# One more VA/GA pair by block products in the input projection of a hybrid decoder trunk

## The chip, the cores and the metric

The kernel runs on one core of one Trainium2 chip. The metric is device time in microseconds for one execution. TensorE (PE) does the matmuls; its weight loads are counted as PEld. VectorE (DVE) and ScalarE (ACT) work element by element, GpSimd (POOL) issues the DMAs that add to what is in memory already, and SyncE (SP) issues nearly all other DMAs. Each engine, and each queue of DMA issues, works through its own instructions in order.

## The reference

One layer over 1024 positions of width 1024, in float32. A projection `w_in` of 7168 columns is cut into six parts, of which `va` and `ga` (1024 columns each) are what the change is about:

```python
h = rms_norm(x, g_mix[l])
z = jnp.einsum("bsd,de->bse", h, w_in[l]) + b_in[l]
va, ga, xb, gb, sa, sb = jnp.split(z, cuts, axis=-1)

u = va * jax.nn.sigmoid(ga)
u = causal_depthwise_conv(u, conv_a_w[l], conv_a_b[l])      # 31 taps
u = jax.nn.silu(layer_norm(u, ln_g[l], ln_b[l]))
y_a = jnp.einsum("bsc,cd->bsd", u, w_a_out[l])

v = causal_depthwise_conv(xb, conv_b_w[l], conv_b_b[l])     # 4 taps
v = rg_lru(v, ...)                                          # two gates by head, a linear recurrence
y_b = jnp.einsum("bsc,cd->bsd", v * jax.nn.gelu(gb), w_b_out[l])

m = jax.nn.sigmoid(sa) * y_a + jax.nn.sigmoid(sb) * y_b
x = x + jnp.einsum("bsd,de->bse", m, w_o[l])
```

A squared-ReLU MLP of width 4096 and a last RMSNorm follow.

## The kernel before

**Two halves for each operand.** A float32 operand is used as a high part in the matmul's own format and a low part, the rest. A product of two operands takes three matmuls: high·high, high·low, low·high. Splitting costs an ACT copy for the high part and, for the low part, either a DVE subtraction or an ACT copy with a minus sign and a POOL DMA that adds the source (`split_dma`, lines 63 to 68).

**The first part** computes columns of `w_in` in chunks of 128 channels by 1024 positions, in the order of the list `CH`: all of XB (12 chunks), and pairs VA j, GA j for j below `NJ` = 7. A chunk is 8 blocks of depth, 3 matmuls, 2 halves of the positions: 48 matmuls of 128x128 by 512. Between the chunks lie the 16 heads' gate matmuls of the recurrence (four groups of four heads). Step `s` issues chunk `s`, and the work on chunk `s` − 1: for XB the convolution of width 4, for VA and GA the sigmoid (`u_gate`, ACT) and the product (`u_value`, DVE). Every 31-tap convolution is one list of 48 DVE operations (`conv`), which begins with two ACT operations (lines 635, 636).

**The second part** computes the other chunks of `w_in` in pairs of chunks, by Strassen's scheme in Winograd's form: the pair's two channel blocks, the two halves of the depth and the two halves of the positions make a 2 by 2 block product that takes 7 block products in place of 8. A block product is 12 matmuls (`z_mm`). Products 1, 2, 3 use blocks of x as they are, products 4 to 7 use sums of blocks, which are made once, early in the first part (`x_sum`, `x_make`), stored to DRAM, and loaded again late (`x_get` loads both halves of a split sum; `x_raw` loads a sum as it is, into the tile of its low half, and `x_split` then splits it: one ACT copy, one DVE subtraction for each of two blocks of 128x1024). The left operands are blocks and sums of the weights (`z_load`, `z_sums`, `z_lhs`). `ZPAIRS` gives the order of 15 pairs: `s`, `t`, `g` are parts of SA, SB, GB, and `u7` is the pair VA 7, GA 7. `zseq` gives the order of products: (pair, product).

**What sets the order.** The order on each engine is that of the program. Step n of the second part issues, in this order: what ACT and DVE do with the result of product n − 1 (`z_post`) and n − 2 (`z_post2`), product n (PE), the left operand of product n + 4, the weight sums of product n + 5, then what `ZX[n]` lists. DVE work passes through a list (`later`), which is emitted at the end of the step sorted by the time at which the planner takes it to be ready; gaps that the planner's clocks show are filled with taps of a convolution (`fill`). `taps["hold"]` keeps it from starting the next convolution. `XS[s]` lists extra work of the first part's steps.

**The recurrence's last group** (tiles 9, 10, 11) is finished around the border of the two parts: `scan_exp` (ACT: exp and tanh), `scan_root` (ACT: square root), `scan_in` and `scan_tile` (DVE; a scan tile is three long operations).

**Tiles.** Blocks of 128x1024 float32 (the sums, their halves, gates, the convolutions' inputs and results) come from one pool of 37. A DMA or engine that needs a tile waits until one is free.

**After the second part** come the projections `w_b_out`, `w_a_out` and `w_o`, and the MLP. In the first steps of the MLP (`GX`, from line 1690 on) `up_lhs(i, p)` makes a left operand, and `g_post` at line 1395 copies the result of a first product out of PSUM (`u`, `u_late`), before the second product may add to it.

```python
z_get(n - 1, z_post)
z_get(n - 2, z_post2)
...
z_get(n, z_mm)
z_get(n + 4, z_lhs)
if n > 0:
    z_get(n + 5, z_sums)
if n < L:
    for f, *a in ZX.get(n, ()):
        f(*a)
vector_work(clk["P"] - 0.3)
```

Of the kernel before, what the change touches and what calls it, by code (L numbers as in the profile page):

```python
# [31 lines left out]
def trunk_kernel(ctx: ExitStack, tc: tile.TileContext, x, xt_in, xt_eo, vecs, w_in, w_a_out, w_b_out,  # L32
# [383 lines left out]
    VA, GA, XB, GB, SA, SB = 0, 8, 16, 28, 40, 48  # L416
# [150 lines left out]
    def scan_in(ready, *ts):  # L567
        for t in ts:
            later(ready, 1.2, nc.vector.tensor_tensor, gate[1, t], gate[1, t], vt.pop(t), ALU.mult)
# [23 lines left out]
    def u_value(j, psv, ready=0):  # L593
        uv = ut[j].rearrange("p (o n) -> p o n", o=2)
        later(ready, 1.28, nc.vector.scalar_tensor_tensor, uv,
              psv.rearrange("p (n o) -> p o n", o=2), bin_c[:, VA + j:VA + j + 1], uv,
              ALU.add, ALU.mult)
        fresh.append(j)
# [108 lines left out]
        later(at("A", 1.06), 1.2, nc.vector.tensor_tensor, l, l.bitcast(F32), xbh[p][c2].bitcast(F32),  # L707
              ALU.subtract)

    NJ = 7  # L710
    CH = [XB + 0, VA + 0, GA + 0, XB + 1, XB + 2, VA + 1, GA + 1, XB + 3, XB + 4, XB + 5, VA + 2, GA + 2, XB + 6, XB + 7, XB + 8, VA + 3, GA + 3, XB + 9, XB + 10, XB + 11, VA + 4, GA + 4, VA + 5, GA + 5, GA + 6, VA + 6]
    NC1 = len(CH)
    zps = {n: z0[n] for n in range(N0)}
    wraw, wst = {}, {}
# [6 lines left out]
    def vector_work(end):  # L721
        for ready, _, cost, f, a in sorted(todo, key=lambda x: x[:2]):
            dve(cost, ready, f, *a)
        todo.clear()
        taps["wait"] += fresh
        fresh.clear()
        fill(end)
# [10 lines left out]
    def chunk_mm(s, n0, n1, halves=(0, 1), low_last=False):  # L738
# [13 lines left out]

    ZPAIRS = [{"u": lambda i: (VA + i, GA + i)}.get(
        t[0], lambda i, c={"g": GB, "s": SA, "t": SB}.get(t[0]): (c + 2 * i, c + 2 * i + 1))(int(t[1]))
        for t in "s0 s1 g0 g1 g2 s2 s3 u7 g3 g4 g5 t0 t1 t2 t3".split()]
    NZ = len(ZPAIRS)
    zraw, zs, zo, zb = {}, {}, {}, {}
    zn = [0]
# [28 lines left out]
    def z_lhs(i, p):  # L787
# [9 lines left out]
        else:  # L797
# [2 lines left out]
        zo[i, p] = o  # L800


    zseq = [(0, 1), (1, 1), (0, 2), (1, 2), (0, 6), (0, 7), (1, 7), (0, 5), (1, 6), (0, 3), (0, 4),
            (1, 5)]
    for i in range(2, NZ):
        zseq += [(i, 1), (i, 7), (i - 1, 4), (i, 6), (i, 2), (i - 1, 3), (i, 5)]
    zseq[-7:] = [(NZ - 1, p) for p in (1, 7, 6)] + [(NZ - 2, 4), (NZ - 1, 2), (NZ - 1, 5), (NZ - 2, 3)]
    zseq += [(NZ - 1, 3), (NZ - 1, 4)]

# [1 line left out]
    for i in range(2, NZ):  # L811
        n = zseq.index((i, 1))
        ZL[n - 9] = ((z_load, i, 0),)
        ZL[n - (6 if i > 2 else 4)] = ((z_load, i, 1),)
    def z_get(n, f):
# [5 lines left out]
    head_at = {s: n for n, s in enumerate(HS0)}  # L821

    EXP = {head_slot: g for g, head_slot in enumerate(HS0[4 * g + 3] + 1 for g in range(3))}
    RAW = (4, 5)
    XS = {4: ((x_sum, 0),), 5: ((x_make, 0, 5), (x_make, 0, 7)), 6: ((x_make, 0, 6), (x_make, 0, 4), (x_sum, 1)),
          7: tuple((x_make, 1, p) for p in (5, 7, 6, 4)),
          NC1 - 3: ((scan_exp, 3),), NC1 - 2: ((x_get, 0, 6), (x_get, 1, 6)),
          NC1 - 1: ((scan_in, 0, 9, 10, 11), (scan_root, 3), (x_get, 0, 7), (x_get, 1, 7))}
    w_load(3)
    head_w(0)  # L830
    w_load(4)
# [1 line left out]
    with tc.manual_schedule(engines=ENGINES):  # L833
        for s in range(3, NC1):
            w_load(s + 2)
            taps["hold"] = s > NC1 - 4
            begun = clk["P"]
            clk["A"], clk["V"] = max(clk["A"], begun + 0.5), max(clk["V"], begun - 2)

# [165 lines left out]
    def z_h(i, m_, hf):  # L1005
        t = ZPAIRS[i][m_] - GB
        if 0 <= t < 12:
            hb[t, hf] = h = EV(f"hb{t}_{hf}")
            nc.sync.dma_start(h, hd[t, :, HALVES[hf]])
# [23 lines left out]
    def z_post2(i, p):  # L1033
# [3 lines left out]
        elif p == 4:  # L1037
            z_out(i, 1, 0, zb[i, "u"], "c")

    ZX = {0: ((x_raw, 0, 5), (x_raw, 1, 5)), 1: ((later, 0, 4.8, scan_tile, 9),), 2: ((x_split, 0, 5),), 3: ((x_split, 1, 5),),  # L1040
          4: ((later, 0, 4.8, scan_tile, 10), (x_raw, 0, 4), (x_raw, 1, 4)), 6: ((x_split, 0, 4),), 7: ((x_split, 1, 4),),
          9: ((later, 0, 4.8, scan_tile, 11),)}
    H_AT = {2: (0, 0), 5: (1, 1), 3: (0, 1), 4: (1, 0)}
    with tc.manual_schedule(engines=ENGINES):

# [37 lines left out]
        z_get(2, z_lhs)  # L1083
        z_get(3, z_lhs)
        u_value(NJ - 1, zps[NC1 - 1])
        vector_work(clk["V"])
        z_h(0, 0, 0)
        for n in range(len(zseq) + 2):
            for f, *a in ZL.get(n, ()):
                f(*a)  # L1090
            if n >= L:
                for f, *a in ZX.get(n, ()):
                    f(*a)
            taps["hold"] = n < 6
            if n >= 20 and n % 6 == 2:
                sum_up(clk["P"], 1)
            clk["A"], clk["V"] = max(clk["A"], clk["P"] + 0.5), max(clk["V"], clk["P"] - 2)
            z_get(n - 1, z_post)
            z_get(n - 2, z_post2)
            if n + 3 < len(zseq):  # L1100
                i, p = zseq[n + 3]
                if p in H_AT:
                    z_h(i, *H_AT[p])
# [8 lines that stand above are left out]
# [581 lines left out]
    def g_get(n, f):  # L1693
# [31 lines left out]
        3: ((x1_normed, 0, 1), (x1_normed, 1, 1), (g_t, "u", 0, 1), (g_t, "u", 1, 1)),  # L1725
        4: ((g_t, "u", 0, 2), (g_t, "u", 1, 2)), 5: ((g_parts, "u", 6, 0), (up_lhs, 0, 6)),
        6: ((g_parts, "u", 6, 1), (up_lhs, 1, 6), (g_parts, "u", 5, 0), (up_lhs, 0, 5)),
        7: ((g_parts, "u", 5, 1), (up_lhs, 1, 5), (g_t, "u", 0, 3), (g_t, "u", 1, 3)),
        9: ((g_parts, "u", 7, 0), (up_lhs, 0, 7)), 10: ((g_parts, "u", 7, 1), (up_lhs, 1, 7)),
        11: ((g_parts, "u", 3, 0), (g_t, "u", 0, 4), (g_parts, "u", 3, 1), (g_t, "u", 1, 4))}.items()})  # L1730
    with tc.manual_schedule(engines=ENGINES):
        for j in range(8):
# [162 lines left out]
    with tc.manual_schedule(engines={mybir.EngineType.Activation, mybir.EngineType.DVE,  # L1895
                                     mybir.EngineType.PE}):
        for n in range(len(useq)):
# [4 lines left out]
            while ready < min(len(useq), n + look + 1):  # L1902
                i, p = useq[ready]
# [289 lines left out]
```

## Time and profile before

| | us |
|---|---|
| median of 3 runs | 1542.22 |
| lowest and highest | 1541.28, 1542.23 |
| the profiled execution, its own time | 1542.07 |
| its span, first to last instruction | 1540.30 |
| PE busy | 1530.1 |
| DVE busy | 1228.9 |
| ACT busy | 911.2 |
| POOL busy | 184.7 |

Times in the views count from the start of the span. The first part runs to about 339 us, the second from there to about 627 us. A row of a timeline gives the start, the length, the engine, the line, the operation, the tiles (out<-in), the shapes and a count; in square brackets stands how long the engine was idle before it, and what ended that. A row of the chain gives start, length, and the work that the end of the program hung on at that time. In the list of waits the numbers are the total in us, the number of waits, and the longest. A window's row gives the busy time of PE, PEld, DVE, ACT and POOL with their counts of instructions, the granted clock of PE, the mean busy share of the DMA engines and GB/s.

### The profile page before, as it was taken

Reading aid. Unit: us, or ns where it says so; the run is one execution under the profiler, and the core shown is the slowest. Engines: PE = TensorE matmul, PEld = TensorE weight load, DVE = VectorE, ACT = ScalarE, POOL = GpSimd, SP = SyncE. Lnnn points to the kernel's source line nnn. Section 1 sums busy time; section 2 is a strip of 40 time slices with the busy share of each in tenths; the row PEclk is TensorE's granted clock in tenths of the full one; section 3 lists DMA queues with packets and bytes.
Section 4 is the critical chain, followed back from the end, with each engine's and each line's share of the span. In section 5 each row is a group of like instructions: output and inputs, shape, how many; then the busy total and the mean of one; then the engine's idle time right before and its main releaser. Section 6 shows DMA issues by size and latency. Waiting matters only on the chain.

```text
span 1540.3 us, 19049 instructions
## 1 busy us (share of the span) xinstructions
PE 1530.1 (99%) x6765; PEld 1258.2 (82%) x6765; DVE 1228.9 (80%) x1660; ACT 911.2 (59%) x1270; POOL 184.7 (12%) x221
## 2 busy tenths in 40 slices
PE   9999999999999999999999999999999999999998
PEld 7888888788888888888888887888888888888886
DVE  6999988989999998478568879765555558888897
ACT  6758576667676676435375777444444475555553
POOL 0000000012222221000022332000000011111110
PEclk9999999999999999999999999999999999999999
DMA  7575554699998888844579898523333779888852
GB/s 295 115 235 149 149 145 116 159 280 244 255 249 214 219 225 253 272 172 128 187 194 304 191 194 201 195 82 132 114 116 108 241 212 232 223 225 222 204 125 110
DMA packets 133504, 296.02 MB, mean 192 GB/s; under 512 B 20896, under 2 KB 38944, under 8 KB 133408
## 3 DMA queue, kind: packets, MB, share of 16 engines
q1 hardware_dynamic: 102016, 215.10, 41.5%
q0 software_dynamic: 30672, 77.35, 27.5%
q10 hardware_dynamic: 720, 2.36, 0.4%
q8 instruction: 53, 0.87, 0.2%
q14 instruction: 43, 0.35, 0.1%
HBM read 155.03 MB, written 60.82 MB: 140 GB/s over the span
## 4 chain that ended last, share of the span: by engine, by line
PE 97%; DMA 1%; ACT 1%; DVE 1%; issue 0%; SPq 0%; POOL 0%; DVEq 0%; POOLq 0%; ACTq 0%
PE z L749 16%; PE d L1946 15%; PE yb L1165 8%; PE e L2063 3%; PE keep L1946 2%; PE z L257 2%; PE rg L529 1%; PE rg L531 1%; PE rg L530 1%; DMA w_raw<-in_w_dram 1%; DMA xc<-in_xt_dram 0%; PE z4a L948 0%; PE go2e L1341 0%; PE z4e L948 0%; PE z2e L948 0%; PE z3e L948 0%
## 5 line engine op out<-in xcount | busy, mean ns | idle before, releaser
L749 PE MATMUL z<-xh,win_h 128*128 128x512 f32 x368 | 115.0, 390 | 0.0
L1958 DVE TENSOR_TENSOR acc<-acc,d 128x1024 f32<-128x1024 f32 x72 | 87.8, 1220 | 33.4 <-PE d L1946 32.7
L749 PE MATMUL z<-xl,win_h 128*128 128x512 f32 x368 | 113.5, 389 | 0.0
L749 PE MATMUL z<-xh,win_l 128*128 128x512 f32 x368 | 91.8, 391 | 0.0
L653 DVE SCALAR_TENSOR_TENSOR y<-u,vec,y 128x511 f32<-128x511 f32 (+14 forms) x120 | 88.4, 737 | 0.0
L653 DVE SCALAR_TENSOR_TENSOR y<-yt,csum,y 128x511 f32<-128x511 f32 (+6 forms) x112 | 82.6, 738 | 0.0
L653 DVE SCALAR_TENSOR_TENSOR yt<-u,vec,yt 128x511 f32<-128x511 f32 (+6 forms) x112 | 82.6, 737 | 0.0
L749 PEld LDWEIGHTS z<-xh,win_l 128*128 128x128 f32 x368 | 69.1, 188 | 15.6
L749 PEld LDWEIGHTS z<-xh,win_h 128*128 128x128 f32 x368 | 69.0, 188 | 15.3 <-ACT win_h L68 0.4
L541 ACT ACTIVATE g<-rg,vec 96x1024 f32<-96x1024 f32 x32 | 35.7, 1115 | 77.0 <-PE rg L531 76.3
L749 PEld LDWEIGHTS z<-xl,win_h 128*128 128x128 f32 x368 | 69.1, 188 | 14.6
L1623 ACT ACTIVATE o<-s 128x512 fp32r<-128x512 f32 x58 | 34.7, 624 | 54.6 <-DVE s L1608 24.5
L475 DVE SCALAR_TENSOR_TENSOR v<-xb,vec,v 128x1023 f32<-128x1023 f32 (+2 forms) x36 | 46.2, 1283 | 14.8 <-ACT v L466 13.9
L67 POOL DMA_DIRECT2D win_l<-win_raw x23 | 19.9, 867 | 306.9 <-ACT win_l L66 245.7
L67 POOL DMA_DIRECT2D zo<-zw x42 | 36.3, 863 | 130.6 <-ACT zo L66 108.0
L1165 PE MATMUL yb<-hgh,wb_h 128*128 128x512 f32 x168 | 51.7, 389 | 0.0
L1165 PE MATMUL yb<-hgl,wb_h 128*128 128x512 f32 x168 | 51.7, 389 | 0.0
L67 POOL DMA_DIRECT2D db_1l<-wr x7 | 6.1, 865 | 309.9 <-DMA wr<-in_w_dram 254.2
L1165 PE MATMUL yb<-hgh,wb_l 128*128 128x512 f32 x168 | 41.0, 389 | 0.0
L66 ACT ACTIVATE zo<-zw 128x512 fp32r<-128x512 f32 x42 | 26.3, 626 | 21.5 <-issue 6.6
L1129 DVE TENSOR_TENSOR o<-s,o 128x512 fp32r<-128x512 f32 x58 | 38.8, 683 | 0.0
L1172 DVE TENSOR_TENSOR sb<-yb,sb 128x512 f32<-128x512 f32 x16 | 10.3, 685 | 34.4 <-PE yb L1165 34.4
(1826 smaller groups left out, 4750.7 us busy)
## 6 DMA issues: line engine op xcount, KB each, us to landing
w_raw<-in_w_dram SPq DMA_DIRECT2D x36, 512.0 KB, 5.7
fr<-fd SPq DMA_DIRECT2D x32, 512.0 KB, 5.7
wr<-in_w_dram SPq DMA_DIRECT2D x32, 512.0 KB, 6.6
zw<-in_w_in_dram SPq DMA_DIRECT2D x30, 512.0 KB, 6.7
win_raw<-in_w_in_dram SPq DMA_DIRECT2D x23, 512.0 KB, 4.5
win_l<-win_raw POOLq DMA_DIRECT2D x23, 512.0 KB, 4.6
zo<-zw POOLq DMA_DIRECT2D x42, 256.0 KB, 5.9
gates<-zg SPq DMA_DIRECT2D x32, 256.0 KB, 3.8
```

What stands on the lines that cost most here:

```text
L67: nc.gpsimd.dma_start(l, src, accum_op=ALU.add)
L257: nc.tensor.matmul(z0[i][:, HALVES[hf]], w0[i][w][:, k, :], xpart(a, hf, k), start=k == 0 and which == "hh", stop=k == 7 and which == ("hl ...
L475: nc.vector.scalar_tensor_tensor(v[:, d:S], a[:, 0:S - d], cbw_c[:, w * 12 + t:w * 12 + t + 1], v[:, d:S], ALU.mult, ALU.add)
L541: nc.scalar.activation(a, gps.pop((n, gi))[:HD, :], AF.Sigmoid, bias=(ba_c, bx_c)[gi][:, n:n + 1])
L653: nc.vector.scalar_tensor_tensor(o[:, k:], a[:, 0:HS - k], c, o[:, k:], ALU.mult, add)
L749: nc.tensor.matmul(zps[s][:, HALVES[hf]], w[:, k, :], xw[k][part][hf], start=n == 0, stop=n == 23)
L1129: tt(l, src, h.bitcast(F32), ALU.subtract)
L1165: nc.tensor.matmul(ps[hf], a, b[:, HALVES[hf]], start=n == 0, stop=n == len(todo) - 1)
L1623: nc.scalar.activation(o[:, 0], src, AF.Copy)
L1946: nc.tensor.matmul(o, a, b, start=n == 0 and (p != 1 or g == 0), stop=n == len(todo) - 1, skip_group_check=p == 1 and g > 0)
L1958: tt(acc[p, q2], acc[p, q2], ps, ALU.add)
L2063: nc.tensor.matmul(o, a, b, start=n == 0 and t < 7, stop=n == len(todo) - 1, skip_group_check=t == 7)
```

## The change

- `NJ` is 6: the chunks VA 6 and GA 6 go from the first part. It ends with GA 5, VA 5 in that order, has 24 chunks in place of 26, and its last step is the one with the last head.
- `ZPAIRS` has 16 pairs: `u6` (VA 6, GA 6) comes seventh, and `u7` moves to tenth place, behind `g3`.
- `zseq`: the first pair's product 4 moves from place 10 to place 13, behind products 1 and 7 of the third pair.
- Product 7's sums are stored as sums (`RAW`), loaded by `x_raw` in the last step of the first part, and split in steps 0 and 1 of the second. Product 5's are loaded ahead of step 0 and split in steps 4 and 5 (before: 2 and 3). Product 4's are loaded in step 6 (before: 4), and split in steps 10 (second block) and 11 (first block) (before: 6 and 7).
- The last group of the recurrence: exp and tanh of tiles 9 and 10 in the step before the last of the first part, those of tile 11 in step 2, the square roots in step 7 (before: the last step of the first part), the scan tiles in steps 8, 11 and 14 (before: 1, 4 and 9).
- The left operand (1, 5) of the MLP moves from `GX` step 7 to 9.
- The steps in which no new convolution may start are now the last of the first part, and 0 to 4 of the second (before: the last three, and 0 to 5).

```diff
-    NJ = 7
-    CH = [..., XB + 11, VA + 4, GA + 4, VA + 5, GA + 5, GA + 6, VA + 6]
+    NJ = 6
+    CH = [..., XB + 11, VA + 4, GA + 4, GA + 5, VA + 5]
...
-        for t in "s0 s1 g0 g1 g2 s2 s3 u7 g3 g4 g5 t0 t1 t2 t3".split()]
+        for t in "s0 s1 g0 g1 g2 s2 u6 s3 g3 u7 g4 g5 t0 t1 t2 t3".split()]
...
-    zseq = [(0, 1), (1, 1), (0, 2), (1, 2), (0, 6), (0, 7), (1, 7), (0, 5), (1, 6), (0, 3), (0, 4),
-            (1, 5)]
+    zseq = [(0, 1), (1, 1), (0, 2), (1, 2), (0, 6), (0, 7), (1, 7), (0, 5), (1, 6), (0, 3), (1, 5)]
     for i in range(2, NZ):
-        zseq += [(i, 1), (i, 7), (i - 1, 4), (i, 6), (i, 2), (i - 1, 3), (i, 5)]
+        zseq += [(i, 1), (i, 7)] + [(0, 4)] * (i == 2) + [(i - 1, 4), (i, 6), (i, 2), (i - 1, 3), (i, 5)]
...
-    RAW = (4, 5)
+    RAW = (4, 5, 7)
...
-          NC1 - 3: ((scan_exp, 3),), NC1 - 2: ((x_get, 0, 6), (x_get, 1, 6)),
-          NC1 - 1: ((scan_in, 0, 9, 10, 11), (scan_root, 3), (x_get, 0, 7), (x_get, 1, 7))}
+          NC1 - 2: ((scan_exp, 3, (0, 1)),),
+          NC1 - 1: ((x_get, 0, 6), (x_get, 1, 6), (x_raw, 0, 7), (x_raw, 1, 7), (scan_in, 0, 9, 10))}
...
-            taps["hold"] = s > NC1 - 4
+            taps["hold"] = s in range(23, 99)
...
-    ZX = {0: ((x_raw, 0, 5), (x_raw, 1, 5)), 1: ((later, 0, 4.8, scan_tile, 9),), 2: ((x_split, 0, 5),), 3: ((x_split, 1, 5),),
-          4: ((later, 0, 4.8, scan_tile, 10), (x_raw, 0, 4), (x_raw, 1, 4)), 6: ((x_split, 0, 4),), 7: ((x_split, 1, 4),),
-          9: ((later, 0, 4.8, scan_tile, 11),)}
+    ZX = {0: ((x_split, 0, 7),), 1: ((x_split, 1, 7),), 2: ((scan_exp, 3, (2,)),),
+          4: ((x_split, 0, 5),), 5: ((x_split, 1, 5),), 6: ((x_raw, 0, 4), (x_raw, 1, 4)), 7: ((scan_root, 3),),
+          8: ((later, 0, 4.8, scan_tile, 9),), 11: ((x_split, 0, 4), (later, 0, 4.8, scan_tile, 10)),
+          10: ((x_split, 1, 4),), 14: ((later, 0, 4.8, scan_tile, 11),)}
...
         u_value(NJ - 1, zps[NC1 - 1])
+        scan_in(0, 11)
         vector_work(clk["V"])
+        x_raw(0, 5)
+        x_raw(1, 5)
...
-            taps["hold"] = n < 6
+            taps["hold"] = n in range(0, 5)
...
-        7: ((g_parts, "u", 5, 1), (up_lhs, 1, 5), (g_t, "u", 0, 3), (g_t, "u", 1, 3)),
-        9: ((g_parts, "u", 7, 0), (up_lhs, 0, 7)), 10: ((g_parts, "u", 7, 1), (up_lhs, 1, 7)),
+        7: ((g_parts, "u", 5, 1), (g_t, "u", 0, 3), (g_t, "u", 1, 3)),
+        9: ((up_lhs, 1, 5), (g_parts, "u", 7, 0), (up_lhs, 0, 7)), 10: ((g_parts, "u", 7, 1), (up_lhs, 1, 7)),
```

More of the change, by code (lines that the diff above doesn't have):

```diff
@@ L708, in x_split @@
               ALU.subtract)
-    NJ = 7
-    CH = [XB + 0, VA + 0, GA + 0, XB + 1, XB + 2, VA + 1, GA + 1, XB + 3, XB + 4, XB + 5, VA + 2, GA + 2, XB + 6, XB + 7, XB + 8, VA + 3, GA + 3, XB + 9, XB + 10, XB + 11, VA + 4, GA + 4, VA + 5, GA + 5, GA + 6, VA + 6]
+    NJ = 6
+    CH = [XB + 0, VA + 0, GA + 0, XB + 1, XB + 2, VA + 1, GA + 1, XB + 3, XB + 4, XB + 5, VA + 2, GA + 2, XB + 6, XB + 7, XB + 8, VA + 3, GA + 3, XB + 9, XB + 10, XB + 11, VA + 4, GA + 4, GA + 5, VA + 5]
     NC1 = len(CH)
```

## The prediction

> **What bounds the kernel now.** I read the page first (busy times, then the chain that ended last). Then came the chain in order of time around the change, the waits of PE, and last the timelines of ACT, DVE, POOL and SP there, with the DMA landings. The page's first and fourth parts:
>
> ```profile
> PE 1530.1 (99%) x6765; PEld 1258.2 (82%) x6765; DVE 1228.9 (80%) x1660; ACT 911.2 (59%) x1270; POOL 184.7 (12%) x221
> PE 97%; DMA 1%; ACT 1%; DVE 1%; issue 0%; SPq 0%; POOL 0%; DVEq 0%; POOLq 0%; ACTq 0%
> ```
> The chain in order of time (start, length, what), then two waits, from the weight loads' timeline and from the list of PE's waits:
> ```profile
> 314.57 24.81 PE z L749 x108
> 339.39 2.72 PE z0a L948 x12
> 342.33 2.72 PE z1a L948 x12
> 358.65 2.72 PE z0e L948 x12
> 366.81 2.72 PE z0f L948 x12
> ```
> ```profile
> 328.21 0.30 PEld L749 LDWEIGHTS z<-xh,win_h 128*128 128x128 f32 x2 [0.42 <-ACT win_h L68]
> PE gu4a L1341 <- ACT u_late L1395: 0.6, 1, 0.6
> ```
>
> TensorE is busy 99% of the span and makes up 97% of the chain: the count of matmuls sets the time, and all else matters only where it makes PE wait. A block product is 12 matmuls in 2.72 us, and products follow each other without a gap. Between the first two stands one extra matmul: 342.33 − 339.39 − 2.72 = 0.2 us.
>
> **The matmuls.** The piece of 24.81 us holds the last 12 matmuls of the chunk before (2.72 us) and the 96 of the two chunks that go, with their wait of 0.42: 24.81 − 2.72 = 22.09 us. Seven products take 7 × 2.72 = 19.04. The gain is **3.05 us**, all on the path. What remains is to ask what is late in the second part, which now begins at 314.57 + 2.72 = 317.3. Product number n starts at 317.5 + 2.72 n where nothing waits.
>
> **ACT ahead of the second part.** ACT's timeline (start, length, line, operation, in brackets the idle time before it), one row of POOL's, one of SP's, and the time to landing of the two DMAs that POOL issued at 329 to 331:
>
> ```profile
> 300.88 1.11 ACT L541 ACTIVATE g<-rg,vec 96x1024 f32<-96x1024 f32 x1 [5.57 <-PE rg L531]
> 301.89 0.80 ACT L635 ACTIVATE y<-u,vec 128x512 f32<-128x512 f32 x1
> 315.74 1.28 ACT L556 ACT_TABLE_LOAD   x1
> 323.86 1.28 ACT L589 ACT_TABLE_LOAD   x1
> 326.17 1.05 ACT L66 ACTIVATE win_l<-win_raw 128x1024 fp32r<-128x1024 f32 x1
> 328.06 0.62 ACT L66 ACTIVATE zo<-zw 128x512 fp32r<-128x512 f32 x1
> 330.14 1.10 ACT L589 ACTIVATE u<-z,vec 128x1024 f32<-128x1024 f32 x1
> 331.27 1.28 ACT L564 ACT_TABLE_LOAD   x1
> 332.56 2.96 ACT L564 ACTIVATE g<-g 128x1024 f32<-128x1024 f32 x3
> ```
> ```profile
> 329.12 1.76 POOL L67 DMA_DIRECT2D zo<-zw  x2 [0.75 <-ACT zo L66]
> 292.44 11.35 SPq L546 DMA_DIRECT2D g<-g  x6
> DMA to landing us min/median/max: 6.2/7.1/7.9
> ```
>
> Differences of starts give the prices: a table load 1.3 (331.27 to 332.56); exp or tanh 1.14 (six and a load between 315.74 and 323.86); a table and a sigmoid 2.3 (323.86 to 326.17); a half-tile copy 0.52 (four between 328.06 and 330.14); three roots with their table 4.2. The exp work of tiles 9 and 10 now follows the gate at 300.88: 301.9 + 1.3 + 4 × 1.14 = 307.8. Then come the first two taps of a convolution (L635 and its neighbour, 1.4), the sigmoid table and the last head's gate (2.3), and only at 311.5 the copies of the first left operands. Their low halves go on by POOL, 1.1 us after the copy begins (328.06, 329.12). So the first lands at 311.5 + 1.1 + 6.2 = 318.8, and PE wants it with its third matmul, at 317.8: 1.0 late, between 0 and 2.7 (7.9 to landing). Before, copy and product lay 11 us apart.
>
> **ACT and DVE during products 0 to 13.** Two rows of ACT, four of DVE, the busy times of two windows (PE, PEld, DVE, ACT, POOL, each with its count; then clock, DMA share, GB/s) and the landing of a weight load that met no other:
>
> ```profile
> 345.09 0.58 ACT L1014 ACTIVATE z1b<-z1a 128x512 f32<-128x512 f32 x1 [1.60 <-PE z1a L948]
> 345.58 0.62 ACT L794 ACTIVATE zo<-zs 128x512 fp32r<-128x512 f32 x1
> 346.10 1.05 ACT L706 ACTIVATE xb5h<-xb5l 128x1024 fp32r<-128x1024 f32 x1
> 348.47 0.69 ACT L973 ACTIVATE zg<-z0a,vec 128x512 f32<-128x512 f32 x1
> ```
> ```profile
> 343.11 1.22 DVE L573 SCALAR_TENSOR_TENSOR g<-a,g 128x1024 f32<-128x1024 f32 x1
> 347.96 0.67 DVE L452 TENSOR_TENSOR zo<-zs,zo 128x512 fp32r<-128x512 f32 x1
> 352.94 1.22 DVE L452 TENSOR_TENSOR xb5l<-xb5l,xb5h 128x1024 fp32r<-128x1024 f32 x1
> 361.24 1.22 DVE L452 TENSOR_TENSOR xb4l<-xb4l,xb4h 128x1024 fp32r<-128x1024 f32 x1
> ```
> ```profile
> 320.00:326.00 6.00, 6.00 (x28) 4.97 (x27) 2.29 (x4) 5.91 (x6) 0.00 (x0) 1.00 1.01 405
> 339.40:368.00 28.60, 28.60 (x127) 23.66 (x127) 28.09 (x32) 20.30 (x33) 4.34 (x5) 1.00 0.87 227
> zw<-in_w_in_dram SPq DMA_DIRECT2D x1, 512.0 KB, 4.6
> ```
>
> In these 28.6 us ACT was busy 20.3, so 8.3 were free. The change puts 11.2 into them: product 7's two splits (2.1), tile 11's exp work and table (3.6), the roots and theirs (4.2), one sigmoid table more (1.3). Product 4's splits only move three to five steps. ACT is full here, and its queue says when the right operands are ready.
>
> Product 7's blocks come first. SP is through with the last head's DMAs at 292.44 + 11.35 = 303.8. The first weight load lands 4.6 later, at 308.4; every further 512 KB takes 1.3 at 405 GB/s. Three more weight loads, two stores, four blocks of product 6, the first of product 7 and 1.3 for POOL's two halves make eleven: 322.7. ACT has done its copies at 318.7 and stands. From 322.7 I add up its queue as the program writes it (evacuation 0.5, half-tile copy 0.52, sigmoid 0.6, split of a block 1.05). Both splits of 7 and four short operations, the exp block, the sigmoid table and two sigmoids, three copies, a split of 5, two evacuations, two copies, the other split of 5: 338.6. Its subtraction on DVE (1.22) ends at 339.8. Product 5 is n = 7 and wants that block half-way, at 317.5 + 19.04 + 1.6 = 338.1: PE is 1.7 us behind, the first 1.0 included.
>
> Then: three copies, the roots, an evacuation, a copy, two evacuations, the sigmoid table and a sigmoid, two copies, a sigmoid, two copies, the second block of 4. That is 352.0 on ACT, 353.2 on DVE. Only behind it does DVE's order have the scan of tile 10 (343.11 to 347.96, 4.85), an addition (0.67) and the first block of 4 (1.22): 359.9. Product 4, n = 13, wants this at 317.5 + 35.36 + 0.2 = 353.1. **PE is then 6.8 us behind in all**, and with no idle time later it never catches up.
>
> The low end comes from margins alone. Before, block 5 was done at 354.2 for a product at 358.65; it is split two steps later now, and 4.5 − 5.44 is 0.9 late. Block 4 was done at 362.5 for 366.81; one step less and a scan ahead of it give 4.3 − 2.72 − 4.85, 3.3 late. If DVE finds room for the scan sooner, nothing is lost. The high end is 9.3, below. I take 6.8, as the queue's rows give it.
>
> **The late operand.** ACT's timeline again:
>
> ```profile
> 946.31 0.62 ACT L66 ACTIVATE o<-s 128x512 fp32r<-128x512 f32 x1
> 947.83 0.58 ACT L1395 ACTIVATE u_late<-gu4a 128x512 f32<-128x512 f32 x1
> 949.85 0.63 ACT L66 ACTIVATE o<-s 128x512 fp32r<-128x512 f32 x1 [0.49 <-DVE s L1611]
> 950.90 0.58 ACT L1395 ACTIVATE u_late<-gu5a 128x512 f32<-128x512 f32 x1
> ```
>
> Two copies (946.31, 1.04 together) move from ahead of the first of these evacuations to behind it. The first comes 1 us sooner and ends the 0.6 us wait. The second stays behind an operand that waits for DVE until 949.85, and PE needs both in order. I take 0, between −1.2 (twice the wait, for both evacuations) and 0. The moved operand's own product comes after both, so nothing waits for it.
>
> **At no price.** The pair's sums, additions and multiplications, some nine DVE operations of 0.7, push the convolutions later:
>
> ```profile
> 595.00 0.69 DVE L660 TENSOR_TENSOR y<-y,yt 128x511 f32<-128x511 f32 x1
> 665.97 1.88 DVE L452 TENSOR_TENSOR q<-q,mu 128x512 f32<-128x512 f32 x3 [4.93 <-PE mu L1194]
> ```
>
> The last one ends at 595, its mean is used at 665, so 20 us later still serves; without that cover PE would wait by what is missing. The two more changes between gelu and sigmoid (tables of 1.3) and the pair's evacuations lie in ACT's 41% of idle time. Two chunk loads with their POOL halves go, and two weight loads come: SP's queue is no longer. Product 7 stores and loads two blocks less.
>
> **Sum.** The profiled run took 1542.07 (span 1540.30), 0.15 under the median of 1542.22. 1542.07 − 3.05 + 6.8 + 0 = **1545.8 us**.
>
> The Trainium skill ("ScalarE: Activation LUTs", What ACT_TABLE_LOAD costs) makes a switch 1.28 us of load and 1.38 of drain. The trace disagrees: the next operation starts 1.3 after the load. By the page, four switches ahead of block 4 would add 5.4, an estimated 1551.2; the row decides.
>
> **Rivals.** *Shorter waits.* By the margins 3.3 are lost, by the queue with product 7's blocks there in time about 5: 1542.3 to 1544.0, taken as 1543.2. For it speaks that two chunk loads leave the DMA queue. *Nothing waits*, the other side: block 7 lies ready at 318.7 and DVE does the scan ahead of step 11. 1542.07 − 3.05 = 1539.0 is left, 1537.8 with the late operand's 1.2. It decides when the queue is 6.8 us shorter than I add up; DVE's 28.09 of 28.6 us speak against it. *The tiles run out*, from SP's waits:
>
> ```profile
> SPq L698 <- DVE g L452: 11.9, 1, 11.9
> ```
>
> SP already stood 11.9 us for a tile of the pool of 37. I count 36 held when block 4 is loaded, so its second load waits for the scan of tile 9 (about 345 to 347), and the weights of pair 2 behind it land 4.6 to 7.1 later. DVE sums these ahead of the scan of 10, up to 2.5 us later than above: 9.3 lost, 1548.3. *The clock falls* in the wait of 5 us at product 4:
>
> ```profile
> 1530.00:1540.00 10.00, 2.94 (x13) 2.08 (x12) 4.98 (x15) 1.78 (x6) 0.00 (x0) 0.76 0.28 105
> ```
>
> Only here, where PE was busy 2.94 of 10 us, is the granted clock under full (0.76). Four us at half clock do the work of two: 1547.8. The rule is the Trainium skill's ("TensorE: Matmul & The Clock Gate", Part 1): half clock after an idle window of some 3.4 us; no row here shows one wait doing it.
>
> **Chances.** Forecast 0.28, tiles 0.10, clock 0.06: slower, 0.44. Shorter waits 0.35: within 0.2% (3.1 us, about what a measurement of this kernel can tell from no change). Nothing waits 0.21: faster. The forecast's own range is 1544.5 to 1547.5; over all cases, with a tenth left out at each end, 1538.3 to 1550.0.
>
> **What would show it.** Right: no wait for win_h; PE waiting at its first product (for a zo DMA), in z0e for xb5l, and longest in z0f for xb4l, with a scan just ahead of that subtraction on DVE; ACT idle 4 us ahead of xb7h; gu5a still waiting for u_late. Wrong, step by step: xb7l landing by 319, the scan of tile 10 ahead of PE's step 11, or no wait in z0f.

## The result and the profile after

The changed kernel takes 1567.54 us (median of 4 runs, 1562.99 to 1569.94), the kernel before 1542.22 beside it (1541.28 to 1543.0): a ratio of 1.0163, with a 95% interval of 1.015 to 1.0176. It is slower, as forecast, but by 25 us in the median and not by 3.6. The profiled run is the lowest of the four: 1562.99, span 1561.2, 20.9 us more than before. All rows below are of this run; what the others lost beyond it, 4.6 us in the median, is in no trace and stays open.

TensorE's list of waits in the changed kernel (what waits, for what: us in total, times, longest), its rows of 0.6 us and more behind the first part (z0a, z0b, z0e, z0f are accumulators of pair 0, zo is a left operand, zc a copy of z0e; xb7h and xb7l are the high and low half of product 7's right operand, xb4h and xb4l those of product 4's):

```profile
PE z0a L947 <- ACT z0b L1013: 6.8, 1, 6.8
PE z0f L947 <- DVE xb4l L452: 6.1, 1, 6.1
PE z0a L947 <- DMA zo<-zw: 1.7, 1, 1.7
...
PE gu4a L1344 <- ACT u_late L1398: 1.1, 1, 1.1
...
PE z0e L947 <- ACT zc L1024: 0.6, 1, 0.6
```

Before, only the 0.6 at gu4a stood there. The wait for win_h is gone, as foreseen, and the first product waits for its operand (1.7). The longest wait, 6.8 us in z0a, is one that the prediction does not have at all. Windows of the changed kernel (busy us of PE, PEld, DVE, ACT, POOL, each with its count; then granted clock, DMA share, GB/s):

```profile
322.00:331.00 9.00, 2.48 (x11) 1.71 (x10) 0.22 (x1) 1.31 (x2) 0.00 (x0) 0.93 1.06 338
331.00:336.70 5.70, 5.41 (x13) 4.25 (x14) 5.67 (x8) 5.64 (x8) 0.00 (x0) 0.51 0.55 219
336.70:364.90 28.20, 27.56 (x121) 22.16 (x119) 23.23 (x32) 24.75 (x37) 5.20 (x6) 1.00 0.61 163
364.90:371.60 6.70, 0.53 (x2) 0.22 (x2) 6.57 (x8) 1.72 (x4) 0.00 (x0) 0.68 0.64 159
371.60:377.00 5.40, 5.40 (x13) 4.29 (x14) 0.85 (x2) 1.93 (x5) 1.72 (x2) 0.50 0.88 198
```

Each long wait is followed by a stretch in which the granted clock is 0.5 and 13 matmuls take the time of 24. The loss in the span adds up so: 16.6 us more in the list of waits (17.2 in all, less 0.6 before), 5.8 for the half clock (5.46 us for a product behind the first wait; 5.06 for 11 matmuls and 3.2 for a product behind the second; 2.72 for 12 matmuls is the rule), less the 3.05 of the matmuls and 0.5 by which the first part ended sooner. That is 18.9 of 20.9; 2.0 us are not in this list.

How the two waits come about stands in the chain of the changed kernel in order of time (start, length, what):

```profile
311.94 17.74 DMA xb7l<-xsd
...
330.66 0.59 ACT z0b L1013
...
331.29 5.46 PE z0a L947 x12
336.75 2.73 PE z1a L947 x12
...
353.89 0.33 SPq L702
...
354.26 4.78 DMA zw<-in_w_in_dram
...
359.13 0.70 DVE zs L452
...
363.82 1.14 DVE xb4l L452
364.96 1.14 DVE g L573
...
370.38 1.15 DVE xb4l L452
...
371.57 5.06 PE z0f L947 x11
```

and in ScalarE's timeline around the first wait (in brackets the idle time before, and what ended it):

```profile
318.75 0.61 ACT L68 ACTIVATE zo<-zs 128x512 fp32r<-128x512 f32 x1
329.69 1.06 ACT L706 ACTIVATE xb7h<-xb7l 128x1024 fp32r<-128x1024 f32 x1 [10.33 <-DMA xb7l<-xsd]
330.66 0.58 ACT L1013 ACTIVATE z0b<-z0a 128x512 f32<-128x512 f32 x1
```

ScalarE stands 10.33 us before the split of product 7's first block. Behind that split in its order is the copy of z0a into z0b, 0.58 us long, which needed no more than product 1. Product 2 adds into z0a and may do so only behind the copy. So a block that TensorE needs as its sixth product stopped the third. VectorE, too, stands for that block (9.68 us). The lower half of the chain is the second wait: the scan of tile 10 (from 364.96) stands between the two subtractions of product 4's low half.

### The profile page after: what moved, and what is told of

Its sections match the earlier page's. It is cut to its first block, busy times and chain, and to the rows that moved or that the text cites. A ratio compares the mean times of both kernels' runs of the same rounds, so it can differ in the third digit from the quotient of the medians.

```text
span 1561.2 us, 19093 instructions
## 1 busy us (share of the span) xinstructions
PE 1533.9 (98%) x6753; PEld 1259.5 (81%) x6753; DVE 1231.6 (79%) x1664; ACT 927.1 (59%) x1295; POOL 191.6 (12%) x229
## 4 chain that ended last, share of the span: by engine, by line
PE 89%; DVE 4%; DMA 3%; ACT 3%; issue 1%; SPq 0%; DVEq 0%; ACTq 0%
PE d L1949 15%; PE z L749 11%; PE yb L1168 8%; PE e L2066 3%; PE keep L1949 2%; PE z L257 2%; DMA xb7l<-xsd 1%; PE rg L531 1%; PE rg L529 1%; PE rg L530 1%; DVE y L653 1%; DMA zo<-zw 1%; PE z0f L947 0%; DVE v L475 0%; DMA w_raw<-in_w_dram 0%
## 5 line engine op out<-in xcount | busy, mean ns | idle before, releaser
L749 PE MATMUL z<-xh,win_h 128*128 128x512 f32 x336 | 105.0, 390 | 0.0
L749 PE MATMUL z<-xl,win_h 128*128 128x512 f32 x336 | 103.7, 389 | 0.0
L749 PE MATMUL z<-xh,win_l 128*128 128x512 f32 x336 | 84.2, 391 | 0.0
L749 PEld LDWEIGHTS z<-xh,win_l 128*128 128x128 f32 x336 | 63.1, 188 | 14.4
L749 PEld LDWEIGHTS z<-xh,win_h 128*128 128x128 f32 x336 | 63.1, 188 | 13.7
L749 PEld LDWEIGHTS z<-xl,win_h 128*128 128x128 f32 x336 | 63.1, 188 | 13.3
L67 POOL DMA_DIRECT2D zo<-zw x47 | 40.6, 864 | 168.7 <-ACT zo L66 120.6
L67 POOL DMA_DIRECT2D zo<-zs x32 | 27.7, 865 | 93.0 <-ACT zo L66 87.6
```

What stands on the lines that cost most here:

```text
L67: nc.gpsimd.dma_start(l, src, accum_op=ALU.add)
L749: nc.tensor.matmul(zps[s][:, HALVES[hf]], w[:, k, :], xw[k][part][hf], start=n == 0, stop=n == 23)
```

## The experiments

Theory: the loss is two waits of order (a split waiting for its data ahead of the copy into z0b; the scan of 10 ahead of xb4l), each with a stretch at half clock, on top of transfers that land later than I added up. Rivals: the data are too late whatever the order is; the tiles hold product 4; something other than standing still makes the matmuls slow.

**The two orders, alone and together.** The first run moves the splits of product 7, the second the scans, the third does both.

```diff
-    ZX = {0: ((x_split, 0, 7),), 1: ((x_split, 1, 7),), 2: ((scan_exp, 3, (2,)),),
+    ZX = {2: ((scan_exp, 3, (2,)),), 3: ((x_split, 0, 7), (x_split, 1, 7)),
```


> The two splits of product 7's right operand go from steps 0 and 1 of the second part to step 3, so that in ScalarE's order the copy of z0a into z0b no longer stands behind a split whose data land at 329.69 us. Nothing else is touched; the loads stay where they were. Theory 'order' (the 6.8 us at step 2 are a copy queued behind a split that waits for a transfer, and the half clock after it is its consequence): the wait of z0a for z0b is under 1 us, the granted clock stays at 1.00 through 331 to 336.5 us, and the time falls by 6.8 + 2.7 = 9.5, less up to 1.5 for product 7, which PE now reaches at about 332 with its halves split at 331 to 333: 1553.5 to 1555 beside 1563.0. Rival 'late transfer' (the data themselves are too late, whatever stands behind them): the wait appears again at step 5 for xb7h or xb7l with 4 us or more, and the time is 1558 or more. The wait for xb4l stays at about 6 by both.


```diff
-          ... 11: ((x_split, 0, 4), (later, 0, 4.8, scan_tile, 10)),
-          10: ((x_split, 1, 4),), 14: ((later, 0, 4.8, scan_tile, 11),)}
+          ... 11: ((x_split, 0, 4),), 13: ((later, 0, 4.8, scan_tile, 10),),
+          10: ((x_split, 1, 4),), 15: ((later, 0, 4.8, scan_tile, 11),)}
```


> The scan of tile 10 goes from step 11 to step 13 and that of tile 11 from step 14 to step 15, so that VectorE does the two subtractions of product 4's low half ahead of the scan. Theory 'scan ahead': the 6.1 us of z0f for xb4l are the scan (4.9 us) with what waits behind it; they fall under 1.5 us and the half clock from 371.5 to 377 us goes with them: 6.1 + 2.6 less up to 1.5, so 1554 to 1557 beside 1563.0. Rival 'second load late' (the second half of product 4's right operand is issued only at 353.9 and would hold the product anyway): the wait stays above 4 us with the load or the split as releaser, and the time is 1560 or more. The wait of z0a for z0b stays at about 6.8 by both.

> Both moves together. If the two waits and the two stretches at half clock are all that the prediction missed, the time is 1563.0 - 9.5 - 8.7 = 1544.8, and with up to 3 us for what is late next 1544.8 to 1547.8: still above the 1542.2 of the kernel before. Rival 'given back': each delay hides the next, the moves don't add, and the time stays above 1550.

Splits moved: 1556.62 us (1553.97 to 1560.23), ratio 1.0095 (1.0079 to 1.0111). Scans moved: 1562.06 (1560.06 to 1562.96), 1.0127 (1.0112 to 1.0142). Both: 1553.74 (1551.91 to 1556.76), 1.0071 (1.0054 to 1.0087). The list of waits, first with the splits moved, then with the scans moved (yb is the projection behind the second part, hgh the high half of its operand):

```profile
PE z0f L947 <- DVE xb4l L452: 6.5, 1, 6.5
PE yb L1168 <- ACT hgh L1068: 2.0, 1, 2.0
...
PE z0f L947 <- DVE xb7l L452: 0.8, 1, 0.8
```
```profile
PE z0a L947 <- ACT z0b L1013: 7.1, 1, 7.1
PE z4a L947 <- DMA zo<-zw: 2.1, 1, 2.1
PE z0f L947 <- DVE xb4l L452: 1.9, 1, 1.9
PE z15e L947 <- ACT zc L1024: 1.5, 1, 1.5
```

Each move takes away its own wait and leaves the other: 6.8 to none, with 0.8 late at product 7; 6.1 to 1.9. The order did it both times; once it is changed, late data and the tiles can explain no more than the 0.8 and the 1.9 that stay. SyncE's wait for a tile is in each of these traces, in the changed kernel so:

```profile
SPq L702 <- DVE g L575: 12.1, 1, 12.1
```

With the scans moved it is 12.3, and product 4 waits 1.9 all the same. In the changed kernel VectorE stood only 0.46 us for the weights behind that load (ahead of the sums at 359.13), and ScalarE went on to the split of the block itself (361.43) without a pause. So the tiles are not what held product 4.

But the time falls by less than the waits. From the profiled 1563.0 I had expected 1553.5 to 1555 with the splits moved, 1554 to 1557 with the scans moved, and 1544.8 to 1547.8 with both; all three came out higher. The traces are of the highest of the four times in each of the three runs (1560.23, 1562.96, 1556.76). With both moves others have taken the place of the two waits:

```profile
PE z4a L947 <- DMA zo<-zw: 2.9, 1, 2.9
PE z0f L947 <- DVE xb4l L452: 2.3, 1, 2.3
PE yb L1168 <- ACT hgh L1068: 1.6, 1, 1.6
```

The half clock has not gone either. With the scans moved it follows the wait of 1.9 us (below, the row of that window in the form used above: a mean clock of 0.76), and with both moves it stands at 0.50 from 408.5 to 412.0, at the end of and behind the wait at z4a, and from 647.5 to 650.9, behind that at yb:

```profile
365.00:372.00 7.00, 4.94 (x14) 3.50 (x13) 6.87 (x9) 3.69 (x7) 1.93 (x3) 0.76 1.04 231
```

The rival "given back" was the better guess for both together: transfers and the other engines did not come sooner with TensorE.

**Is it standing still that halves the clock?** 26 matmuls on an operand long at hand are put into the first wait, with the order left as changed.

```diff
-        ps = z_bank(i, b) if p in (1, 7) else zb[i, b]
+        ps = z_bank(i, b) if p in (1, 7) and (i, p) != (0, 7) else zb[i, b]
...
+        if (i, p) == (0, 2):
+            idle = z_bank(0, "f")
+            for _ in range(26):
+                nc.tensor.matmul(idle, xh[0][0][:, 0:P], xh[0][0][:, 0:HS], start=True, stop=True)
```


> 26 matmuls on an operand long at hand are put ahead of product 2 of the first pair, into a bank that is not used until product 7; they cost some 5.9 us (26 x 0.227) inside a wait of 6.8, and are extra work whose result is overwritten. Theory 'clock' (the two products after the wait take 5.4 us each where 2.72 is the rule, because TensorE stood still before them and was granted half the clock): the granted clock in 331 to 336.5 us is 1.00, product 2 takes 2.7, and the time falls by 2.7 to about 1560.3. Rival 'something else makes them slow' (the transfers or the loads of weights in that stretch): they stay at 5.4 us in spite of the filled wait and the time stays at 1563, or rises by what the extra matmuls overrun.

The windows at the place of the first wait:

```profile
322.00:331.00 9.00, 8.77 (x39) 6.94 (x37) 0.00 (x0) 0.92 (x1) 0.00 (x0) 1.00 1.07 333
331.00:336.70 5.70, 5.03 (x22) 4.14 (x23) 5.50 (x8) 5.64 (x9) 0.00 (x0) 1.00 0.59 236
```

The clock is 1.00, and 22 matmuls go where 13 went, at nearly the same DMA share (0.59 beside 0.55). So the half clock is a consequence of the wait. The Trainium skill ("TensorE: Matmul & The Clock Gate", Part 1) says that an idle window of some 3.4 us brings half clock; the 6.8 and 6.1 us here agree, and with the wait filled it stays away. The time, though, is 1563.65 (1562.89 to 1564.49), 1564.49 in the profiled run against 1562.99, where I expected 1560.3: z4a, z2e, z0e and keep (an accumulator of the MLP) now wait 3.3 us longer in all, more than the 2.7 gained, and the second stretch at half clock is there as before. The rest of the 1.5 us is in no row.

**The pace of the transfers.** The first four left operands of the second part are split by ScalarE and VectorE alone; once with the order as changed, once with both moves.

```diff
-        if p in (7, 5) or conv_over():
+        if p in (7, 5) or zn[0] < 5 or conv_over():
```


> The changed kernel, with nothing done but the first four left operands of the second part split by ScalarE and VectorE alone, so that GpSimd's accumulating transfers at 310 to 318 us are gone; the order of ScalarE stays as changed, with product 7's split ahead of the copy into z0b. Theory 'shared pace, then order': the loads land 1.3 us apart, product 7's first half lands at 323.3 instead of 329.7, its split ends at 324.4 and the copy at 324.9; PE reaches product 2 at 322.7 and waits 2 to 2.5 us instead of 6.8, which is too short for the half clock; the 1.7 us at the first product go too: 1.7 + 4.5 + 2.7 = 8.9 less, 1554 beside 1563.0 of the profiled run. Rival 'order alone': the copy still waits until about 328 to 330, the wait stays above 5 us, and the time above 1560. The wait for xb4l stays at 6 by both.

> Both moves of order, and the first four left operands of the second part are split by ScalarE and VectorE alone, so the four accumulating transfers that GpSimd issues at 310 to 318 us are gone; VectorE gets four passes of 0.69 us more. In the changed kernel the loads of product 6 land 2.6 us apart, each with one accumulating transfer landing between them. Theory 'shared pace' (loads and accumulates take turns on the same DMA engines): without the accumulates the loads land 1.3 us apart, product 7's first half lands 5 us earlier, at about 324 to 325 instead of 329.7, and the wait of the first product for its operand (1.2) goes: 1550.5 to 1553 beside 1553.7. Rival 'the order of the queue sets it' (the loads stand behind one another whatever else runs): product 7 lands at 328 or later, and the time is 1553 to 1556.

With the order as changed 1559.55 us (1557.3 to 1561.93), ratio 1.0117 (1.01 to 1.0134); the profiled run took 1557.95, where I expected 1554. With both moves 1552.21 (1549.46 to 1554.16), 1.0059 (1.0044 to 1.0075), which the spread does not tell from the 1553.74 of the two moves alone. Queues and transfers issued from 306 to 320, in the changed kernel (packets, MB, share of the 16 engines' time; then count, KB each, median us to landing):

```profile
q1 hardware_dynamic: 1512, 3.94, 78.3%
q0 software_dynamic: 266, 0.50, 19.3%
...
zo<-zw POOLq DMA_DIRECT2D x4, 256.0 KB, 8.4
xb7l<-xsd SPq DMA_DIRECT2D x2, 512.0 KB, 17.8
```

and with both moves and without the accumulates:

```profile
q1 hardware_dynamic: 1798, 4.98, 96.9%
...
xb7l<-xsd SPq DMA_DIRECT2D x2, 512.0 KB, 11.4
```

The accumulating transfers take 19.3% of the time for 0.50 MB, the loads 78.3% for 3.94: by these shares one of 256 KB costs the loads about as much as another 512 KB, an estimate. Without them the first block of product 7, issued at 311.9 in both, lands 6.4 us sooner. In the run with the order as changed the first wait is then 2.1 us instead of 6.8, with the clock at 1.00 behind it: lateness and order are two factors of one wait, and either takes most of it away.

**Product 7 whole.** One part of the change undone: the right operand of product 7 stored and loaded as high and low part again, so that the second part has no split of it.

```diff
-    RAW = (4, 5, 7)
+    RAW = (4, 5)
-          ... (x_raw, 0, 7), (x_raw, 1, 7), (scan_in, 0, 9, 10))}
+          ... (x_get, 0, 7), (x_get, 1, 7), (scan_in, 0, 9, 10))}
-    ZX = {0: ((x_split, 0, 7),), 1: ((x_split, 1, 7),), 2: ((scan_exp, 3, (2,)),),
+    ZX = {2: ((scan_exp, 3, (2,)),),
```


> The changed kernel with product 7's right operand again stored and loaded as high and low part (four loads of 512 KB instead of two), and so without its two splits in the second part; the rest is as in the changed kernel. Theory 'order': no split stands before the copy into z0b any more, so the wait of 6.8 us at step 2 is gone as with the moved splits; the two more loads land some 2 x 1.3 to 2 x 2.6 us later, at 333 to 336, and product 7, which PE reaches at 332, waits 1 to 4 us; the wait for xb4l stays about 6: 1554 to 1558 beside 1556.6 with the moved splits alone. Rival 'tiles' (the two more buffers are not free so early and hold SP's queue): the loads of product 7 are issued only after 316 and product 7 waits over 5 us: 1559 or more.

1554.2 us (1553.61 to 1554.34), ratio 1.0073 (1.0058 to 1.0088): 13.3 us less than the changed kernel in the median, from one part. The waits:

```profile
PE z0f L947 <- DVE xb4l L452: 6.0, 1, 6.0
PE z0a L947 <- DMA zo<-zw: 2.3, 1, 2.3
```

No wait for z0b and none for xb7, where I expected 1 to 4 us, although two loads more are in the queue: ScalarE has nothing late to wait for. The tiles rival had product 7 wait over 5 us; it falls.

**The late operand.** Alone in the kernel before, and taken back beside both moves.

```diff
-        7: ((g_parts, "u", 5, 1), (up_lhs, 1, 5), (g_t, "u", 0, 3), (g_t, "u", 1, 3)),
-        9: ((g_parts, "u", 7, 0), (up_lhs, 0, 7)), ...
+        7: ((g_parts, "u", 5, 1), (g_t, "u", 0, 3), (g_t, "u", 1, 3)),
+        9: ((up_lhs, 1, 5), (g_parts, "u", 7, 0), (up_lhs, 0, 7)), ...
```


> The kernel before with one part of the change alone: the left operand of product 5 at step 9 instead of 7. Theory 'operand costs': gu4a waits for u_late 1.0 to 1.3 us instead of 0.59, gu5a 0.2, and the time rises by 0.5 to 0.9 to about 1543. Rival of the prediction (nothing, or down to -1.2): the wait is 0.6 or less and the time 1541 to 1542.3.

> Both moves of order, and the left operand of product 5 back at step 7 instead of 9. The prediction gave the later operand 0 us (bounds -1.2 to 0). In the changed kernel gu4a waits for u_late 1.08 us where it waited 0.59 before, and what follows gu5a has fallen 0.7 us further behind. Theory 'operand costs': with the operand back the wait is 0.6 again and the time 0.7 us less than with the two moves alone (1553.7), 1553.0. Rival 'the wait only moved with the stages before it': the wait stays above 1.0 and the time at 1553.7. Three rounds cannot tell 0.7 us in the time; the rows decide.

Alone: 1542.01 us (10 runs, 1541.01 to 1543.37), ratio 0.9996 (0.9987 to 1.0006): nothing, as predicted, and my expectation of 0.5 to 0.9 more was wrong. The copy out of gu4a came 1.0 us sooner (946.80 instead of 947.83) and that out of gu5a at 950.90 as before, as the prediction has it. But gu4a's wait did not end: it is 0.8 instead of 0.6, since TensorE came to it 1.2 us sooner as well. Taken back: 1551.07 (1549.59 to 1558.58), and gu4a still waits 1.2, beside 1.4 with the two moves alone. So the wait above 1 us is there with the operand in either place; the difference to 1553.74 lies inside the spread of these runs.

**Can the pair bring its 3.05 us?** Six runs put edits together. "Four edits" are both moves of order, the first operands without accumulates, and (0, 4) and (1, 4) behind (1, 3). With product 7 whole, no split is left to move. In some the two VA/GA pairs go to places 5 and 8, and in the last two more operands, (2, 6) and (2, 3), go to ScalarE and VectorE.

```diff
-        zseq += [(i, 1), (i, 7)] + [(0, 4)] * (i == 2) + [(i - 1, 4), (i, 6), (i, 2), (i - 1, 3), (i, 5)]
+        zseq += [(i, 1), (i, 7)] + ([(1, 3), (0, 4), (1, 4), (2, 6), (2, 2), (2, 5)] if i == 2 else
+                                    [(i - 1, 4), (i, 6), (i, 2), (i - 1, 3), (i, 5)])
-        for t in "s0 s1 g0 g1 g2 s2 u6 s3 g3 u7 g4 g5 t0 t1 t2 t3".split()]
+        for t in "s0 s1 g0 g1 u6 g2 s2 u7 s3 g3 g4 g5 t0 t1 t2 t3".split()]
-        if p in (7, 5) or zn[0] < 5 or conv_over():
+        if p in (7, 5) or zn[0] < 5 or (i, p) in ((2, 6), (2, 3)) or conv_over():
```


> Both moves of order and the first left operands without accumulates as before, and the product (0, 4) and (1, 4) one product later, behind (1, 3). With the two moves and without accumulates the profiled run had 2.4 us of wait for xb4l. Theory 'xb4l is late by a fixed time': the later place takes 2.7 us from it and the wait goes, the time falls by up to 2.4 from 1549.5 of the profiled run (1552.2 median): 1547 to 1550. Rival 'given back': the waits behind it (z2e, z15e and yb for ScalarE's copies and for transfers, 4.6 us together) grow by what is gained, and the time stays at 1549.5 to 1552.5.

> As the run with four edits, and the two VA/GA pairs earlier in the second part (places 5 and 8 instead of 7 and 10), so that VectorE gets the convolutions of their channels sooner. Before, VectorE's last convolution pass ran at 587.9 us, 39 us ahead of the end of the second part, and ScalarE and VectorE alone made the left operands from there on; in the changed kernel it runs at 622.7, 24 us ahead of the end, and GpSimd's transfers go on into the stage that loads hg. Theory 'convolutions end late': earlier pairs end them earlier, the waits of yb for hgh and hgl and of z15e for zc (2.8 us together) shrink to under 1, and the time falls by 1.5 to 3. Rival 'VectorE is full anyway' (busy 93 of 100 us from 450 to 600): the last pass is not earlier by more than 3 us, and the time within 1 us of the run with four edits.

> Product 7's right operand loaded whole as before, so without its splits, with the scan behind, without the first accumulates and with (0, 4) later. Without the accumulates its four loads land 1.3 us apart, from about 323 to 328, ahead of PE at 331, and ScalarE and VectorE have 2.1 and 2.4 us less to do in the stretch. Theory 'the sums of 7 cost what they ask of ScalarE and VectorE': no wait for xb7 is left (1.3 us less than in the run with four edits) and the time is 1545.5 to 1549. Rival 'not bound there': the time is that of the run with four edits within 1 us.

> The run with product 7 whole and the other edits (1546.0 median, 1545.2 profiled), and with it the left operand of product 5 back at step 7 and the two VA/GA pairs at places 5 and 8. Theory 'the pair is worth its 3.05 us once no wait is left': these two edits take gu4a's wait from 1.1 to about 0.6 and some of 0.5 to 1.0 at z4a and keep, so 1543.5 to 1545.5, and the kernel before (1542.3) is not beaten, since z2e and z2b still wait 1.6 us for transfers. Rival 'other waits take their place': the time stays at 1546 or more.

> The run with product 7 whole, the scan behind and (0, 4) later, but with the first four left operands split by accumulating transfers as in the changed kernel. It tells what those transfers cost when product 7 is not in danger. Theory 'shared pace': the first product waits 1.7 to 2.3 us for its operand and the loads of product 7 land at 330 to 334 with 0 to 1.5 us of wait; 1547.5 to 1549.5 beside 1546.0. Rival 'no cost once the order is right': 1546.5 or less.

> As the run with all these edits and early pairs, with two more left operands, (2, 6) and (2, 3), split by ScalarE and VectorE in place of accumulating transfers, since z2b and z2e wait 0.8 us each for such a transfer. Theory 'transfers late': both waits go and the time is 1.0 to 1.6 us lower than without this edit, 1542 to 1544.5. Rival 'VectorE has no room' (busy 14.7 of 15 us from 350 to 365): the waits become waits for VectorE, of the same size or larger, and the time is the same or higher.

| run | us, median (range) | ratio (95%) |
|---|---|---|
| four edits | 1551.56 (1549.72 to 1552.63) | 1.006 (1.0045 to 1.0075) |
| and pairs early | 1550.27 (1548.68 to 1550.9) | 1.0051 (1.0036 to 1.0066) |
| four edits, product 7 whole | 1546.02 (1544.24 to 1546.86) | 1.0021 (1.0012 to 1.0031) |
| that, pairs early, operand back | 1546.83 (1545.49 to 1549.37) | 1.0033 (1.002 to 1.0046) |
| product 7 whole, with accumulates | 1550.31 (1549.86 to 1550.65) | 1.0052 (1.0037 to 1.0067) |
| as the fourth, two more operands | 1546.09 (1543.88 to 1548.81) | 1.0025 (1.0015 to 1.0035) |

The later place of (0, 4) takes the wait for xb4l away, and the time stays: given back. Whole blocks for product 7 bring 5.5 us more; here the theory held and its rival fell. The accumulates cost 4.3 us even with product 7 whole, more than I expected (1.5 to 3.5); the first product waits 2.4 for one, and the clock is halved behind that. Pairs early and two more operands change nothing beyond the spread, as their rivals had it for the time. The mechanism of the last rival is not what the row shows, though: z2f waits 1.7 us for another transfer and only 0.6 for VectorE. My theory that convolutions which end late hold up hg fell by a row. With product 7 whole the last passes of the convolution run as late as this, and no wait for hg is left:

```profile
L653 DVE SCALAR_TENSOR_TENSOR y<-yt,csum,y x58: 730/739/747, 402.8 to 639.9; 128x499 f32<-128x499 f32 x5, 128x498 f32<-128x498 f32 x5, 128x511 f32<-128x511 f32 x4, 128x510 f32<-128x510 f32 x4
```

The best of them is still 3.6 us above the 1542.4 measured beside it. Its waits behind the first part:

```profile
PE gu4a L1345 <- ACT u_late L1399: 1.1, 1, 1.1
PE keep L1950 <- DVE fb L1674: 0.9, 1, 0.9
PE z2e L948 <- DMA zo<-zs: 0.8, 1, 0.8
PE z2b L948 <- DMA zo<-zs: 0.8, 1, 0.8
PE z0e L948 <- ACT zc L1025: 0.6, 1, 0.6
PE z4a L948 <- DMA zo<-zw: 0.5, 1, 0.5
```

4.7 us in these rows, where the kernel before had 0.6: the 3.05 of the matmuls are spent on small waits for ScalarE, VectorE and transfers. When one group was taken away (z2e and z2b in the last run) that wait at z2f came in its place. Whether a version with the pair can be faster than before stays open; none of these is.

## Why the prediction was wrong

- **The matmuls, −3.05.** The wait for win_h is gone and 96 matmuls are replaced by 84. Nothing speaks against the term.
- **The first product, 1.0 (0 to 2.7).** 1.7: right in place, in kind and inside the bounds. The size is in part luck: the copy began at 309.72 instead of 311.5, and the transfer took 8.3 us to landing instead of 6.2.
- **"Eleven: 322.7".** This step failed by 7.0 us: the first block of product 7 landed at 329.7. I counted 1.3 us for "POOL's two halves"; five accumulating transfers run in that stretch, each worth about a load of 512 KB (1.3), so an estimated 5.2 of the 7.0 us were left out here. The run without four of them has the block 6.4 us sooner.
- **"ACT has done its copies at 318.7 and stands."** This is the step that cost most, and it left something out. I let the standing delay only what needs product 7 (n = 7, then 13), and listed the splits and "four short operations" behind them without asking who waits for those. One is the copy into z0b, and product 2 waits for it: ScalarE stood until 329.69, and TensorE 6.8 us. With the splits behind that copy the wait is gone. None of my three signs of being wrong came; this step was not among them.
- **z0e for xb5l, 1.7 behind.** Not seen: TensorE was by then over 11 us behind and found the block ready (0.6 for zc instead).
- **Product 4, the longest wait, with the scan of 10 just ahead.** Right in kind, and close in size: 5.1 of the 6.8 were to arise here, 6.1 did (only the wait at z0b is longer), behind a subtraction at 370.38 and a scan from 364.96. Moving the scan left 1.9. The close size is in part luck: the operand came 11.6 us later than forecast (371.5 instead of 359.9) and TensorE 10.2 us (365.0 instead of 354.8). The path of the *tiles* rival was there as well: the chain goes through SP's load of the second block (353.89), issued only when VectorE had released a tile, and then through the weights of pair 2 to the sums (359.13) ahead of the scan. It held VectorE for 0.46 us, not for the 2.5 of that rival.
- **The clock, a rival at 0.06.** It happened twice and cost 5.8 us. It was no alternative to the forecast but a consequence of it: whoever forecasts a wait of 5 us must add what stands behind it to the sum. The price that I gave it (2 us) was low: 2.7 and 3.1.
- **The late operand, 0.** Right in the time (0.9996 alone) and in what holds the second copy; wrong in that the wait at gu4a would end (0.8).
- **The table switch, "the row decides".** The operation behind the load again starts 1.3 us after the load's start (333.78 to 335.07), so the estimate of 1551.2 falls.
- **"At no price".** In the changed kernel the pair's work on VectorE costs little (yb waits 0.3). It is not free: as soon as the large waits go, small waits on ScalarE, VectorE and transfers appear in the sum that the margins before could not show.
- **The rival "nothing waits".** It fell; no version came below the kernel before.

The direction came from two terms that were right in kind (the first operand, product 4); the missing 17 us of the profiled run are the copy into z0b (6.8), the half clock (5.8), and some 5 us of smaller terms, of which 2.0 have no name.

## What to carry to other kernels

When an engine that works in order is given an instruction that waits for a transfer, list everything behind it in its queue up to the moment the data land, and ask for each who waits for it; the cheapest operation there (0.58 us here) can be the one that stops TensorE. A wait of TensorE of some us has a second price, the matmuls at half clock behind it (2.7 and 3.1 us here), and belongs in the sum with it. A saving of 3 us in matmuls is lost when the work that feeds them gets no slack: without the large waits the kernel came from 1567.5 to 1546.0, and the small ones that were left or came anew still cost more than the saving.

## What the runs showed that I had not expected

An accumulating transfer that GpSimd issues takes twice the DMA time per byte of a load (19.3% for 0.50 MB beside 78.3% for 3.94). And a wait much shorter than 6 us can be followed by half clock. In the run with product 7 whole and the accumulates, the wait was 2.4 us:

```profile
320.00:321.00 1.00, 1.00 (x5) 0.78 (x6) 0.15 (x1) 0.00 (x0) 0.00 (x0) 0.93 1.07 289
321.00:322.00 1.00, 1.00 (x4) 0.81 (x3) 0.00 (x0) 0.00 (x0) 0.00 (x0) 0.50 1.05 305
...
324.00:325.00 1.00, 1.00 (x5) 0.85 (x4) 0.00 (x0) 0.80 (x2) 0.00 (x0) 0.86 1.08 303
```

The clock falls a good 1 us after work has begun again and stays low for some 3.4 us, by the shares in the first and the last of the rows with a part of it. In the changed kernel the two low stretches last some 6.8 and 10.2 us, two and three times as long: by rows of this kind from 329.8 to 336.6 and from 367.3 to 377.6. The first and the last row of the shorter one:

```profile
329.00:330.00 1.00, 0.00 (x0) 0.00 (x0) 0.00 (x0) 0.31 (x1) 0.00 (x0) 0.89 1.02 418
...
336.00:337.00 1.00, 1.00 (x4) 0.76 (x4) 0.96 (x3) 0.97 (x2) 0.00 (x0) 0.70 0.00 0
```

Another wait of 2.4 us (xb4l, with both moves and without accumulates) left the clock at 1.00, and so did one of 2.1; one of 1.9 (with the scans moved) was followed by half clock for 3.4 us. The window of some 3.4 us that the Trainium skill gives ("TensorE: Matmul & The Clock Gate", Part 1) is thus no safe bound from below: waits of about the same length came out both ways.
